# Two more gate units as seven products, the norm weight row from TensorE, u as fp32, cache rows and early loads moved

## The chip, the cores and the metric

The kernel runs on one core of a Trainium2 chip. The metric is the device time of one execution in microseconds (us), as the median of several runs. A core has TensorE (PE in the profile, with its weight loads as PEld), VectorE (DVE), ScalarE (ACT), GpSimd (POOL) and SyncE (SP), which issues most loads; stores are issued by POOL, and data moves over 16 DMA engines.

## The reference

One step of a one-layer streaming encoder over 1,024 prompt frames and 64 sample frames (together T = 1,088 columns), all in fp32:

```
h = rmsnorm(x, g_mix)
cb, cc, ch, q, k, v, ga, gb = split(h @ w_in)   # 3 x 512, 3 x 512, 2 x 1024 columns
u   = cb * causal_conv(cc * ch, state_conv)     # depthwise, width 3
o   = band_attention(q, k, v, rel_bias)         # 8 heads of 64; own 64-frame chunk and 8 before it
mix = sigmoid(ga) * (u @ w_cout) + sigmoid(gb) * (o @ w_ao)
x1  = x + mix @ w_out
y   = rmsnorm(x1 + swiglu(rmsnorm(x1)))         # d_ff = 2816
# further outputs: the new conv state, and the caches of k and v, old rows moved up by 64
```

## The kernel before

**Precision and products.** An fp32 operand is split into a high and a low fp32r half (`split`, L133 to L135: a cast on ACT, then a subtraction on DVE), and a product is three matmuls: high by high, high by low, low by high. Units of 256 columns of w_in are computed in Strassen's way: seven products of half size in place of eight (`STEPS`), each of them 24 matmuls of 272 columns. Class `Unit` loads a unit's raw weights and makes the seven combinations (`prep`), `runner` runs the products, and `results` passes their sums on through copies (`sq`, `sk`, `sg` and so on, L482). The tags A (two places), B and D (one between them, tag BD) are TensorE's PSUM places.

**Stages in order of the program.** (1) The first x tile, the norm weight row `gm_row` and v's weights are loaded; sixteen matmuls on zeros (`wake`, L376) run meanwhile. Each tile of x is squared and summed on ACT (L385), scaled by its norm and by `gm_row` on DVE (L387), turned by TensorE (`xt`, L397), split, and multiplied for v (`pvv`, L430 to L432); q's first unit is begun among these tiles (`q_step`). (2) The list `todo` runs through q0, k0, q1, k1 and cc, ch, cb of both halves, with g0 and g1 (the first four tiles of gate columns, `NG` = 2) among them. `cc_done`, `ch_done` and `cb_done` make the convolution's input `ut`, the convolution (`conv`, whose old contents of `ut` go out as the new conv state) and u, which is written to memory. (3) The other twelve tiles of gate columns (`gates`) are plain products, each four chunks of 24 matmuls (`gate_chunk`, L684 to L686), between the steps of the attention: 8 heads by 9 tiles of queries. One step is the scores `s` (L814, L815), the softmax on DVE (L765) and ACT (L775), for an earlier step the turned weights `t` (L845) and their split `pt`, and for a still earlier one the values `pv` (L871) and their sum (`cb`, `co`, L795 and L796). Scores and turned weights share a PSUM pool of two places. `PER` says how many steps follow a chunk. The last two gate tiles (`BEHIND`) come after the attention and cover the loads of u, o and the row sums r. (4) The merge (`ya` from u, `yb` from o, with the gates), then w_out, the up stage and the down stage, where ACT and DVE work beside long rows of TensorE products.

**What sets the order.** The kernel is written for a scheduler which gives each engine a list of instructions that it works off in order: it takes what is ready by its own estimate, and among that the earlier in the program. Only what is marked so keeps its place in the program (`keep_in_program_order`). An engine that waits at a row holds up all rows behind it on that engine. A buffer of a pool is free when the last reader of its previous contents is done; a load into it is issued only then.

**The rest that the change touches.** The copy of the cache rows (L963) goes from memory to memory on POOL's queue, and the scheduler put its two parts at 8.9 and 42.3 us. u is stored by `cb_done` as two fp32r halves and loaded whole (L926); o and r are loaded in twelve pieces, multiplied (L937) and split. Raw weights share the pool `rpool` with two places.

## Time and profile before

| | |
|---|---|
| median of 3 runs (lowest, highest) | 1539.8 us (1539.04, 1539.97) |
| the profiled execution's own time | 1534.63 us |
| its span, first to last instruction | 1532.8 us |
| mean granted TensorE clock | 0.989 |
| read from and written to memory | 168.86 MB, 89.85 MB |

In a timeline row stand the start, the length, engine, line, operation, output and inputs, the shapes and the number of instructions put together; in brackets is the idle time of that engine ahead of the row and what ended it. A row of a window has, for each engine, its busy time and its number of instructions, then the granted clock, the share of the DMA engines and GB/s. In the chain, a row is a piece of the path that ended last. In a list of groups, behind the bar stand the busy time, the mean of one in ns, and the idle time ahead of them with its cause. The page's second part shows where the program is in time: TensorE is busy in nine tenths or more of nearly every slice but the first.

### The profile page before, as it was taken

How to read it: one execution, taken by the hardware profiler on the slowest of the kernel's cores; microseconds unless marked ns; L12 is line 12 of the kernel's file. 1: busy time of each engine (PE TensorE's matmuls, PEld its weight loads, DVE VectorE, ACT ScalarE, POOL GpSimd, SP SyncE). 2: the span in 40 equal slices, each digit the busy share in tenths (PEclk: the TensorE clock that was granted, in tenths of full speed). 3: DMA queues.
4: the chain of work that ended last, by engine and by line, in shares of the span. 5: the costliest groups of instructions: out<-in, count | busy, mean ns of one | idle time of the engine just before them, and what ended most of it. 6: DMA issues, size and time to landing. Idle time of an engine off the chain costs nothing.

```text
span 1532.8 us, 26063 instructions
## 1 busy us (share of the span) xinstructions
PE 1486.7 (97%) x10002; PEld 1390.1 (91%) x10002; DVE 993.6 (65%) x1893; ACT 686.0 (45%) x1407; POOL 208.3 (14%) x353
## 2 busy tenths in 40 slices
PE   7989998999999999999998999999999999999997
PEld 6789998999999999998888999999999998788886
DVE  6676564555666763666379666666666668857576
ACT  6444432334666663553166444444444445403123
POOL 1234411022222222000200011000010111000000
PEclk9999999999999999999999999999999999999999
DMA  7455522249655627645532344333443438776675
GB/s 251 144 191 188 191 53 87 88 110 302 188 142 158 154 70 259 201 127 161 198 126 74 131 155 154 118 121 124 147 155 141 156 148 309 239 239 225 225 259 199
DMA packets 137868, 257.01 MB, mean 168 GB/s; under 512 B 18432, under 2 KB 76992, under 8 KB 137584
## 3 DMA queue, kind: packets, MB, share of 16 engines
q1 hardware_dynamic: 109264, 167.33, 35.0%
q0 software_dynamic: 27184, 85.40, 15.1%
q10 hardware_dynamic: 1296, 2.62, 0.5%
q8 instruction: 78, 1.28, 0.4%
q14 instruction: 46, 0.38, 0.1%
HBM read 168.86 MB, written 89.85 MB: 169 GB/s over the span
## 4 chain that ended last, share of the span: by engine, by line
PE 84%; DMA 7%; DVE 5%; ACT 3%; issue 1%; SPq 0%; POOL 0%; ACTq 0%; DVEq 0%
PE Aa L261 9%; PE Ab L261 8%; PE A L1480 7%; PE Da L261 4%; PE Db L261 4%; PE D L1480 4%; PE p L686 2%; PE Bb L261 2%; PE Ba L261 2%; PE p L685 2%; PE p L684 2%; PE wo L1045 2%; PE wo L1046 2%; PE wo L1044 2%; PE B L1480 2%; PE Ag L261 2%
## 5 line engine op out<-in xcount | busy, mean ns | idle before, releaser
L1480 PE MATMUL A<-ring,ht 128*128 128x512 f32 x528 | 126.0, 392 | 4.8 <-ACT acc L1490 3.6
L1480 PEld LDWEIGHTS A<-ring,ht 128*128 128x128 f32 x528 | 98.6, 188 | 28.2 <-ACT acc L1490 4.8
L1211 POOL DMA_DIRECT2D h_d<-hq x77 | 41.1, 534 | 412.8 <-DVE hs L135 220.3
L134 ACT CAST ring<-w2r 128x512 fp32r<-128x512 f32 (+1 forms) x78 | 43.6, 589 | 107.4 <-PE A L1480 50.6
L684 PE MATMUL p<-xo,whp 128*128 128x272 f32 x288 | 84.2, 292 | 0.0
L686 PE MATMUL p<-xo,wlp 128*128 128x272 f32 x288 | 83.6, 290 | 0.0
L685 PE MATMUL p<-xo,whp 128*128 128x272 f32 x288 | 83.3, 289 | 0.0
L134 ACT CAST hq<-sa 128x512 fp32r<-128x512 f32 x77 | 47.9, 622 | 75.9 <-DVE sa L1223 57.7
L765 DVE CUSTOM_DVE_ANT_0 p<-s,bias 128x640 f32<-128x640 f32 (+5 forms) x72 | 47.3, 658 | 29.1 <-PE s L815 28.6
L135 DVE TENSOR_TENSOR hq<-sa,hq 128x512 fp32r<-128x512 f32 x77 | 53.0, 689 | 20.0 <-ACT hq L134 19.9
L135 DVE TENSOR_TENSOR wla<-rawa,wha 128x512 fp32r<-128x512 f32 x55 | 37.8, 688 | 41.8 <-ACT wha L134 41.8
L261 PE MATMUL Aa<-mg,wha 128*128 128x272 f32 x352 | 60.3, 293 | 3.9 <-ACT mg L134 3.1
L1480 PE MATMUL D<-ring,ht 128*128 128x512 f32 x264 | 63.9, 394 | 0.0
L1480 PEld LDWEIGHTS D<-ring,ht 128*128 128x128 f32 x264 | 49.5, 188 | 11.9 <-ACT acc L1490 0.4
L261 PE MATMUL Ab<-mg,whb 128*128 128x272 f32 x352 | 58.7, 289 | 0.0
L261 PE MATMUL Ab<-tt,whb 128*128 128x272 f32 x352 | 58.6, 288 | 0.0
L261 PE MATMUL Aa<-tt,wha 128*128 128x272 f32 x352 | 58.6, 288 | 0.0
L134 ACT CAST wha<-rawa 128x512 fp32r<-128x512 f32 x55 | 34.1, 622 | 51.4 <-PE Ab L261 36.8
L135 DVE TENSOR_TENSOR ring<-w2r,ring 128x512 fp32r<-128x512 f32 (+1 forms) x78 | 48.5, 646 | 9.8 <-ACT ring L134 9.6
L261 PEld LDWEIGHTS Aa<-mg,wha 128*128 128x128 f32 x352 | 50.8, 192 | 4.3 <-ACT mg L134 3.4
L684 PEld LDWEIGHTS p<-xo,whp 128*128 128x128 f32 x288 | 54.3, 189 | 0.3
L685 PEld LDWEIGHTS p<-xo,whp 128*128 128x128 f32 x288 | 54.3, 189 | 0.1
(537 smaller groups left out, 4556.5 us busy)
## 6 DMA issues: line engine op xcount, KB each, us to landing
h_d<-hq POOLq DMA_DIRECT2D x77, 512.0 KB, 3.9
ht<-h_d SPq DMA_DIRECT2D x154, 256.0 KB, 3.6
rawa<-in_w_ff SPq DMA_DIRECT2D x11, 1024.0 KB, 5.6
rawb<-in_w_ff SPq DMA_DIRECT2D x11, 1024.0 KB, 4.9
w2r<-in_w_ff SPq DMA_DIRECT2D x11, 1024.0 KB, 4.8
qd<-q_d SPq DMA_DIRECT2D x32, 272.0 KB, 6.2
rawp<-in_w_in SPq DMA_DIRECT2D x6, 1024.0 KB, 8.0
g_d<-gst POOLq DMA_DIRECT2D x24, 256.0 KB, 4.0
```

Of the source, the lines that this page charges most:

```text
L134: act.copy(hi, src)
L135: vec.tensor_tensor(lo, src, hi.bitcast(F32), op=ALU.subtract)
L261: mm(t[:, j, :HN], x[:, k, :], moving(p, l, k, j * HN, HN), start=p in (1, 2, 7) and k == 0 and n == 0, stop=k == 3 and n == 2, skip_group ...
L684: mm(out, a, p, start=g == 0 and k == 0, stop=False)
L685: mm(out, a, q, start=False, stop=False)
L686: mm(out, b, p, start=False, stop=g == last and k == 3)
L765: vec.tensor_tensor_reduce(out=s if len(ps.shape) == 2 else s.rearrange("p (a b) -> p a b", a=2), in0=ps, in1=bias if len(ps.shape) == 2 e ...
L1044: mm(ps, x(k, 0), wh, start=f, stop=False)
L1045: mm(ps, x(k, 0), wl, start=False, stop=False)
L1046: mm(ps, x(k, 1), wh, start=False, stop=e)
L1211: nc.gpsimd.dma_start(h_d[p, c - 1], hq.rearrange("p i l t -> p (i l t)").bitcast(F32))
L1480: mm(t, ht[k][:, j, x], w[:, l], start=p in (1, 2, 7) and k == 0 and n == 0, stop=k == len(ks) - 1 and n == 2, skip_group_check=p in (6, 5 ...
```

## The change

- **Norm weight row.** It is loaded as one row of 4 KB (`gm_one`) instead of 128 copies, multiplied by a column of -0.5 on TensorE (two fp32 matmuls into `gm_ps`, between the wakes) and copied to `gm_row` by ACT. The second x tile is loaded ahead of v's weights.
- **Cache rows.** Their copies are pinned in the up stage.
- **Turned tile 6** gets the PSUM place BD, and q's first two products come one tile later.
- **q1's raw weights** are loaded into a buffer of their own in `cp` (`early`).
- **The convolution** is put into the list of things to be done later, two rounds on for its first half and one for its second.
- **u** is stored and loaded as fp32 and split after the attention. u, o and r are loaded in three chunks of columns for all four row blocks (`chunk`), through two places each; the name `ul` and `ol` share theirs.
- **Gates.** g2 and g3 join `todo` (`NG` = 4). Eight gate tiles stay plain, so `PER` goes from 2.04 to 3.6.

```diff
 C_CB, C_CC, C_CH, C_Q, C_K, C_V, C_GA, C_GB = 0, 512, 1024, 1536, 2048, 2560, 3072, 4096
-PER = 2.04
+PER = 3.6
 WAKE = 16
...
     r_d = dr.tile([NH, T], F32, name="r_d")
-    u_d = dr.tile([4, P, 2, T], F32, name="u_d")
+    u_d = dr.tile([4 * P, T], F32, name="u_d")
     x21_d = dr.tile([P, 2, 4, HT], F32, name="x21_d")
...
     class Unit:
-        def __init__(self, src, nm):
+        def __init__(self, src, nm, place=None):
             self.nm = nm
             self.pool = ws
-            self.raw = rpool.tile([P, KD, 2 * P], F32, tag="raw", name=f"raw{nm}")
+            self.raw = (place or rpool).tile(
+                [P, KD, 2 * P], F32, tag="raw", name=f"raw{nm}", bufs=1 if place else 2
+            )
             nc.sync.dma_start(self.raw, src.rearrange("(k p) n -> p k n", p=P))
...
-    def unit_in(n):
+    def unit_in(n, place=None):
         nm, at, _ = todo[n]
-        return Unit(w_in[:, at : at + 256], nm)
+        return Unit(w_in[:, at : at + 256], nm, place)
...
+        gm_one = ph.tile([P, D], F32, tag="x", name="gm_one", bufs=3)[:1]
         load_x(HORDER[0])
-        gm_row = ph.tile([P, D], F32, name="gm_row", bufs=1)
         gm = ins["g_mix"][0]
-        nc.scalar.dma_start(gm_row, bass.AP(tensor=gm.tensor, offset=gm.offset, ap=[[0, P], [1, D]]))
-        pool_e.tensor_scalar(gm_row, gm_row, -0.5, None, op0=ALU.mult)
+        nc.scalar.dma_start(gm_one, bass.AP(tensor=gm.tensor, offset=gm.offset, ap=[[D, 1], [1, D]]))
+        load_x(HORDER[1])
         wv_raw = []
...
             wv_raw.append(raw)
-            load_x(HORDER[half + 1])
+        load_x(HORDER[2])
         wv = []
...
         wake = psS.tile([P, 512], F32, tag="mm", name="wake")
+        minus_half = ph.tile([P, 2, 4, P], F32, tag="kept", name="minus_half", bufs=4)[:1, 0, 0]
+        vec.memset(minus_half, -0.5)
+        gm_ps = bank2("A", "gm_ps")
         for i in range(WAKE):
+            if i == 4:
+                for j in range(2):
+                    mm(gm_ps[:, j], minus_half, gm_one[:, j * 512 : (j + 1) * 512], start=True, stop=True)
             mm(wake, zero[:, :P], zero, start=True, stop=True)
+        gm_row = ph.tile([P, D], F32, name="gm_row", bufs=1)
...
-        def norm(i):
+        def norm(i, also=None):
...
             act.activation(junk[:n], xt[:n], AF.Square, accum_out=ssq[:n])
+            if also:
+                also()
             r = norm_factor(ph, ssq[:n], n, f"m{i}")
...
             xg = xts.pop(i)
-            pt = bank2("A", f"xt_{i}").rearrange("p a (b t) -> p a b t", t=P)
+            pt = bank2("BD" if i == 6 else "A", f"xt_{i}").rearrange("p a (b t) -> p a b t", t=P)
             for hf in range(2):
...
-        norm(HORDER[0])
+        norm(HORDER[0], lambda: act.copy(gm_row, gm_ps.rearrange("p a b -> p (a b)")))
         norm(HORDER[1])
...
                 q_step = runner(unit, todo[0][2])
-            if n in (5, 6):
-                q_step.products(n - 5)
+            if n in (6, 7):
+                q_step.products(n - 6)
...
         return snap.rearrange("p j n -> p (j n)")
-
-    def staged(nm):
-        return sp.tile([P, 2, HT], F32R, tag="st", name=nm)
...
             if ended[r] == 2:
-                conv(r)
+                late.append([2 - r, lambda: conv(r)])
...
                 vec.tensor_tensor(x[:, a : a + n], x[:, a : a + n], cvo[r][:, col(t) : col(t) + n], op=ALU.mult)
-            st = staged(f"su{c2}_{r}{h}")
-            split(st[:, 0], st[:, 1], x)
+            i = 2 * c2 + r
             for a, t, n in places(h):
-                nc.gpsimd.dma_start(u_d[2 * c2 + r, :, :, t : t + n], st[:, :, a : a + n].bitcast(F32))
+                nc.gpsimd.dma_start(u_d[i * P : (i + 1) * P, t : t + n], x[:, a : a + n])
...
             todo.append((f"{nm}{c2}", base + 256 * c2, (c2, n)))
-    NG = 2
+    NG = 4
+    for m in range(2, NG):
+        todo.append((f"g{m}", C_GA + 256 * m, gate_out(2 * m)))
...
     cvp = k_step = None
+    early = {2: unit_in(2, cp)}
     for n, (nm, at, done) in enumerate(todo):
...
         if n + 1 < len(todo):
-            nxt_unit = unit_in(n + 1)
+            nxt_unit = early.pop(n + 1, None) or unit_in(n + 1)
         for si in range(len(STEPS)):
...
     ob = Acts([uo.tile([P, 2, 4, T], F32R, name="ob")])
-    for i in range(4):
-        nc.sync.dma_start(u.t[0][:, :, i, :].bitcast(F32), u_d[i])
-    with tc.tile_pool(name="ol", bufs=3, reuse_waits="tile") as olp:
-        for i in range(4):
-            for c, (o, n) in enumerate(CH):
-                t = olp.tile([P, 384], F32, tag="ol", name=f"ol{i}_{c}")
-                nc.sync.dma_start(t[:, :n], o_d[i * P : (i + 1) * P, o : o + n])
-                rb = olp.tile([P, 384], F32, tag="rb", name=f"rb{i}_{c}")
-                for j in range(2):
-                    nc.sync.dma_start(
-                        rb[j * HD : (j + 1) * HD, :n], r_d[2 * i + j : 2 * i + j + 1, o : o + n].to_broadcast([HD, n])
-                    )
-                vec.tensor_tensor(t[:, :n], t[:, :n], rb[:, :n], op=ALU.mult)
-                split(ob.at(0, i, o, n), ob.at(1, i, o, n), t[:, :n])
+    with tc.tile_pool(name="ol", bufs=2, reuse_waits="tile") as olp:
+
+        def chunk(src, o, n, nm):
+            t = olp.tile([P, 4, 384], F32, tag="ol", name=f"{nm}_{o}")[:, :, :n]
+            nc.sync.dma_start(t, src[:, o : o + n].rearrange("(i p) t -> p i t", p=P))
+            return t
+
+        for c, (o, n) in enumerate(CH):
+            t = chunk(u_d, o, n, "ul")
+            split(u.four(0, 0, o, n), u.four(0, 1, o, n), t)
+            t = chunk(o_d, o, n, "ol")
+            rb = olp.tile([P, 4, 384], F32, tag="rb", name=f"rb_{o}")[:, :, :n]
+            for j in range(2):
+                nc.sync.dma_start(
+                    rb[j * HD : (j + 1) * HD],
+                    bass.AP(
+                        tensor=r_d.tensor, offset=r_d.offset + j * T + o, ap=[[0, HD], [2 * T, 4], [1, n]]
+                    ),
+                )
+            vec.tensor_tensor(t, t, rb, op=ALU.mult)
+            split(ob.four(0, 0, o, n), ob.four(0, 1, o, n), t)
         for n in range(len(gates) - BEHIND, len(gates)):
...
     wo_raw = []
-    for nm in ("k", "v"):
-        src = ins[f"cache_{nm}"].rearrange("t h d -> t (h d)")
-        nc.gpsimd.dma_start(outs[f"cache_{nm}_sample"][: CACHE - TS], src[TS:])
...
     unit = ub
+    for nm in ("k", "v"):
+        src = ins[f"cache_{nm}"].rearrange("t h d -> t (h d)")
+        tc.keep_in_program_order(nc.gpsimd.dma_start(outs[f"cache_{nm}_sample"][: CACHE - TS], src[TS:]))
     for n in range(1, len(names)):
...
```

ACT's order at the start, rows 4 to 13, before and after; `junk` is the Square of an x tile, `wvh` the high half of v's weights, `kept` and `xo` come from a turned x tile:

```order
4 L385 ACTIVATE junk,ssq_142<-x_109 128x1024
5 L148 ACTIVATE normm_144<-normm_144 128x1
6 L134 CAST wvh_176<-wv_114 128x512
7 L134 CAST wvh_180<-wv_114 128x512
8 L134 CAST wvh_184<-wv_114 128x512
9 L134 CAST wvh_188<-wv_114 128x512
10 L385 ACTIVATE junk,ssq_151<-x_116 128x1024
11 L148 ACTIVATE normm_153<-normm_153 128x1
12 L134 CAST wvh_192<-wv_118 128x512
13 L134 CAST wvh_196<-wv_118 128x512
```

```order
4 L394 ACTIVATE junk,ssq_147<-x_110 128x1024
5 L148 ACTIVATE normm_150<-normm_150 128x1
6 L394 ACTIVATE junk,ssq_157<-x_113 128x1024
7 L456 COPY gm_row<-gm_ps 128x1024
8 L148 ACTIVATE normm_159<-normm_159 128x1
9 L134 CAST wvh_182<-wv_115 128x512
10 L134 CAST wvh_186<-wv_115 128x512
11 L134 CAST wvh_190<-wv_115 128x512
12 L162 COPY kept_175<-xt_166 128x512
13 L134 CAST xo_99<-xt_166 128x4x128
```

The two Squares and the copy of the row now stand ahead of all casts of v's weights, and the first turned tile's copy and cast ahead of the second half of these weights (wv_117).

SP's queue around the load of q1's raw weights, before (rawq_1042) and after (rawq_813); `bt` and `ct` are the bias and cache rows that are loaded behind the last x tile:

```order
13 L354 DMA x_525<-in_x_prompt 128x1024
14 L594 DMA bt<-in_bias_ext 8x768
15 L582 DMA ct_1357<-in_cache_k 128x512
16 L582 DMA ct_1467<-in_cache_k 128x512
17 L595 DMA bias_e<-bt 8x768
18 L194 DMA rawq_1042<-in_w_in 128x8x256
```

```order
13 L356 DMA x_531<-in_x_prompt 128x1024
14 L601 DMA bt<-in_bias_ext 8x768
15 L196 DMA rawq_813<-in_w_in 128x8x256
16 L602 DMA bias_e<-bt 8x768
17 L589 DMA ct_1363<-in_cache_k 128x512
18 L589 DMA ct_1473<-in_cache_k 128x512
```

The load moved ahead of the cache rows and has no earlier reader to wait for.

TensorE in the third head's attention, from the scores of tile 6 to those of tile 7, before and after; `p` are the gates' plain products:

```order
1419 L814 MATMUL s_6_4817<-kd_4309,qd_0_4312 128x320
1420 L815 MATMUL s_6_4817<-kd_4309,qd_1_4315 128x320
1421 L814 MATMUL s_6_4817<-kd_4309,qd_0_4312 128x320
1422 L815 MATMUL s_6_4817<-kd_4309,qd_1_4315 128x320
1423 L845 MATMUL t_4_4826<-ident,p_4_4748 128x128 x5
1424 L871 MATMUL pv_3_4835<-pt_1_4757,vd_4325 128x512 x3
1425 L871 MATMUL pv_3_4835<-pt_1_4757,vd_4325 128x2x128
1426 L684 MATMUL p_0_4873<-xo_99,whp_00_4532 128x272
1427 L814 MATMUL s_7_4847<-kd_4309,qd_0_4312 128x320
```

```order
1425 L696 MATMUL p_3_5193<-x_4100,wlp_00_4313 128x272
1426 L694 MATMUL p_3_5193<-x_4100,whp_00_4312 128x272
1427 L695 MATMUL p_3_5193<-x_4100,whp_00_4312 128x272
1428 L696 MATMUL p_3_5193<-x_4100,wlp_00_4313 128x272
1429 L694 MATMUL p_3_5193<-xo_101,whp_01_4316 128x272
1430 L695 MATMUL p_3_5193<-xo_101,whp_01_4316 128x272
1431 L855 MATMUL t_4_5081<-ident,p_4_5031 128x128 x5
1432 L881 MATMUL pv_3_5090<-pt_1_5040,vd_4664 128x512 x3
1433 L881 MATMUL pv_3_5090<-pt_1_5040,vd_4664 128x2x128
1434 L696 MATMUL p_3_5193<-xo_101,wlp_01_4317 128x272
1435 L694 MATMUL p_3_5193<-xo_101,whp_01_4316 128x272
1436 L824 MATMUL s_7_5129<-kd_4648,qd_0_4651 128x320
```

Before, such a step has one plain matmul in it here, and others (the next of this head) have some twenty; after, each has about eight. Over the whole attention, from the first scores to the last row sum, there are some 885 of them before and 574 after.

## The prediction

> **What bounds the kernel now.** I read the page's busy shares and its chain first, then the rows of TensorE's timeline, looking for places where an idle time stands in brackets behind a row, and last the windows over single stages.
>
> ```profile
> PE 1486.7 (97%) x10002; PEld 1390.1 (91%) x10002; DVE 993.6 (65%) x1893; ACT 686.0 (45%) x1407; POOL 208.3 (14%) x353
> ...
> PE 84%; DMA 7%; DVE 5%; ACT 3%; issue 1%; SPq 0%; POOL 0%; ACTq 0%; DVEq 0%
> ```
>
> TensorE is busy for 1486.7 of 1532.8 us, and 84% of the chain is its own work. So time can go in three ways: fewer TensorE instructions, closing the 46 us in which it stands idle, and raising the clock behind idle places. The profiled run took 1534.63 us, 1.8 more than its span and 5.2 less than the median, 1539.8. I sum differences against the profiled run and take them off the median, since nothing says that the change moves the distance between the two.
>
> **The start** (norm row, order of the loads, cache rows). TensorE's timeline, then other engines' rows of the same time:
>
> ```profile
> 1.48 6.26 PE L376 MATMUL wake<-zero 128*128 128x512 f32 x16 [1.48 <-DVE zero L373]
> 13.12 1.97 PE L397 MATMUL xt<-ident,x 128*128 128x128 f32 x8 [5.38 <-DVE x L387]
> 17.62 0.50 PE L430 MATMUL pvv<-wvh,xo 128*128 128x512 f32 x1 [0.38 <-ACT xo L134]
> 26.10 1.06 PE L397 MATMUL xt<-ident,x 128*128 128x128 f32 x8 [0.75 <-DVE normm L149]
> ```
>
> ```profile
> 5.88 1.06 ACT L385 ACTIVATE junk<-x 128x1024 bf16<-128x1024 f32 x1 [3.22 <-DMA x<-in_x_prompt]
> 6.14 2.78 POOL L360 TENSOR_SCALAR gm_row<-gm_row 128x1024 f32<-128x1024 f32 x1 [3.73 <-DMA gm_row<-in_g_mix]
> 9.97 1.90 DVE L135 TENSOR_TENSOR wvl<-wv,wvh 128x512 fp32r<-128x512 f32 x3 [1.87 <-ACT wvh L134]
> 11.41 1.05 ACT L385 ACTIVATE junk<-x 128x1024 bf16<-128x1024 f32 x1
> 11.79 1.28 DVE L387 SCALAR_TENSOR_TENSOR x<-x,normm,gm_row 128x1024 f32<-128x1024 f32 x1
> 15.33 1.14 ACT L134 CAST wvh<-wv 128x512 fp32r<-128x512 f32 x2 [1.97 <-DMA wv<-in_w_in]
> 16.50 0.59 ACT L162 COPY kept<-xt 128x512 f32<-128x512 f32 x1
> ```
>
> Before, the row is ready at 6.14 + 2.78 = 8.92, the scaling stands on DVE behind three wvl subtractions (to 11.8), and the cast that frees the first v matmul stands on ACT behind two casts that wait for wv's second half (15.33). After, the ACT order is Square of x0, Square of x1, the copy that makes the row, then three casts of wv. Square of x0 ends at about 7 with its accumulator read; Square of x1, whose load is now second, adds 1.05 to 1.4, and the copy of 1024 columns, which the trace does not show, at least 0.59 (half its columns, row at 16.50) and at most 2 x 0.59 = 1.2; I take 1.1, as the Square of 1024 columns takes. The row is there at 9.6 to 9.7. DVE then scales x0 at once (1.28): x0's turn starts at about 11.0 instead of 13.12. Two casts or copies of 0.59 behind its first half put the first v matmul at 13 instead of 17.62. The two fp32 matmuls that make the row are not in the trace: at least the 0.39 of a wake matmul (6.26 / 16), and, if fp32 costs four times that, 1.6 each, 3.2 together. They lie among the sixteen wakes, which have nothing to do before 11.0, and so cost nothing; they even shorten the idle time ahead of the first turn. To these 4.6 us comes the wait of 0.75 at 26.10 for the next tile's norm, whose inputs are earlier too. The term: **-5.4**. Its ends: -2, when wv's second half still lands at 15.3 and the second group of casts waits for it, and -7.5. The queue now carries 1 MB less of other work in those microseconds (the row's 512 KB broadcast, and a cache copy of 896 KB, below), so I take the nearer end to the latter.
>
> **q's two units** (PSUM place of the turned tile, products one tile later, q1's raw weights early). Rows of TensorE's timeline; of the chain; and windows whose next to last figures are granted clock and DMA share:
>
> ```profile
> 63.92 1.38 PE L397 MATMUL xt<-ident,x 128*128 128x128 f32 x8 [3.18 <-DVE x L387]
> 91.09 0.77 PE L261 MATMUL Aq<-xo,whq 128*128 128x272 f32 x4 [1.85 <-ACT whq L134]
> 107.92 0.77 PE L261 MATMUL Aq<-xo,whq 128*128 128x272 f32 x4 [2.65 <-DVE sq L482]
> ```
>
> ```profile
> 71.21 3.00 PE Bq L261 x24
> 77.70 0.87 PE xt L397 x8
> 96.59 9.86 DMA rawq<-in_w_in
> 107.15 0.73 DVE sq L482
> ```
>
> ```profile
> 91.10:95.10 4.00, 3.91 (x17) 3.54 (x18) 4.00 (x7) 2.02 (x4) 2.09 (x4) 0.59 0.81 296
> 107.90:112.60 4.70, 4.68 (x25) 4.68 (x26) 4.37 (x7) 1.85 (x4) 1.46 (x2) 0.64 0.63 207
> 1299.00:1304.00 5.00, 3.26 (x13) 2.17 (x12) 4.71 (x8) 4.71 (x10) 0.00 (x0) 1.00 1.04 408
> ```
>
> Between the last two turned tiles (63.92 and 77.70) the old order has a product of 24 matmuls and 35 of v, some 11 us; the new one has 6 of v and a product, 4.4 us. So the work that ACT and DVE do on the last tile starts some 6 us earlier, more than the 1.85 us that TensorE waited at 91.09, and what is late next is DVE's own queue. The second wait hangs on a load: q1's raw weights were issued only at 96.59, when q0's buffer came free, and landed 9.86 later; DVE stood at the subtraction that reads them, with the one behind it (107.15) that frees TensorE's PSUM. With a buffer of its own the load is the 15th row of SP's queue instead of the 18th and waits for nothing of q0; its 9.86 us then lie beside the last tiles of v, far ahead of 107. I take both waits away, 1.85 + 2.65 = 4.5, and the low clock behind each, 4.0 x 0.41 = 1.6 and 4.7 x 0.36 = 1.7: **-7.8**. Ends: -3, if DVE's queue is late in both places, and -8.5. The wait of 3.18 at 63.92 is for the last x load, which the change leaves where it was: 0.
>
> The row at 1299 has waits of the same size, and its clock stays 1.00; so whether a wait of some 2 us lowers the clock is not fixed by its length. The Trainium skill ("TensorE: Matmul & The Clock Gate", Part 1: The HAM clock gate) puts the halving behind at least one idle window of some 3.4 us that runs freely. By that rule neither wait here should have lowered the clock, and the 3.3 us of the two stretches would stay, for a sum 3.3 higher; the two windows at 0.59 and 0.64 speak against it, the one at 1299 for it.
>
> **The convolution's wait** (it is issued two steps later at most).
>
> ```profile
> 237.78 0.06 DVE L527 MEMSET ut<- 128x2 f32 x1 [8.48 <-DMA out_state_conv_sample<-ut]
> 241.90 1.19 PE L261 MATMUL Ag<-xo,whg 128*128 128x272 f32 x4 [4.08 <-DVE sg L482]
> 241.90:246.50 4.60, 4.60 (x24) 4.60 (x25) 1.78 (x3) 0.00 (x0) 2.18 (x4) 0.63 0.56 178
> out_state_conv_prompt<-ut POOLq DMA_DIRECT2D x4, 1.0 KB, 12.2
> ```
>
> DVE stands 8.48 us at a memset, until a store of the old contents has landed, and TensorE waits 4.08 behind it, with 4.6 x 0.37 = 1.7 of low clock. In the order after, the memset has moved by one row and the stores by as little. A store of 1 KB takes 12.2 us by the median, and nothing shortens it. I take **-0.5**; the ends are 0 and -5.8.
>
> **Gates and attention.** Two more units of 256 columns as seven products: 14 products of 24 matmuls more, 14 x 3.00 = 42.0 us. In return 16 plain chunks of 24 matmuls go.
>
> ```profile
> 364.80:584.40 219.60, 216.99 (x1579) 202.45 (x1578) 150.24 (x376) 149.05 (x353) 49.32 (x91) 1.00 0.54 151
> 584.40:606.30 21.90, 21.90 (x177) 21.87 (x176) 4.11 (x9) 5.28 (x14) 4.85 (x9) 1.00 1.00 356
> L765 DVE CUSTOM_DVE_ANT_0 p<-s,bias 128x640 f32<-128x640 f32 (+5 forms) x72 | 47.3, 658 | 29.1 <-PE s L815 28.6
> L135 DVE TENSOR_TENSOR pt<-t,pt 128x640 fp32r<-128x640 f32 (+2 forms) x64 | 41.8, 652 | 10.1 <-ACT pt L134 9.6
> DVE p L765 <- PE s L815: 28.6, 31, 2.2
> ACT pt L134 <- PE t L845: 17.3, 32, 1.3
> ```
>
> In the second window TensorE does nothing but plain chunks: 21.90 / 177 = 0.124 us a matmul. So 16 x 24 x 0.124 = 47.5 go, 42.0 come: **-5.5**. That is TensorE alone. The plain chunks are also what it does while ACT and DVE turn scores into weights. Of the first window's matmuls some 885 are such filler; after, by the order, 574. The attention's own work is 219.6 - 885 x 0.124 = 109.9 us, 1.5 for each of 72 steps; with 574 x 0.124 = 71.2 of filler the window would be 181 us, 2.5 a step instead of 3.05. DVE's 150.2 and ACT's 149.1 in the window shrink only by the share of the gates (a third of some 11 and 24 us), to 146 and 141: from 68% to 81% and 78% of the window. Both stay below full, and DVE's waits for scores (28.6 us) say that it is TensorE that is late today. But each step is a ring: turn the weights (five transposes), ACT casts, DVE subtracts (0.652), and only then is the PSUM place free for the next but one. I add **+3** for places where this ring is late, between 0 and +10. After the last step 98 filler matmuls (12 us) are left instead of 176 (21.9).
>
> **u and the merge.** u's high and low halves were loaded as written; now u is loaded once, as fp32, and split.
>
> ```profile
> u<-u_d SPq DMA_DIRECT2D x4, 1088.0 KB, 9.4
> 609.58 4.17 DMA rb<-r_d
> 613.88 0.57 DVE ol L937
> L684 PE MATMUL yb<-ob,whm 128*128 128x384 f32 (+1 forms) x96 | 32.2, 337 | 3.4 <-ACT ob L134 3.4
> 615.00:619.00 4.00, 3.96 (x13) 3.97 (x14) 2.49 (x6) 0.97 (x2) 0.00 (x0) 0.50 0.57 150
> ```
>
> Today the merge waits 3.4 us for o and loses 4.0 x 0.50 = 2.0 by the clock behind it. After, half of u's 4.4 MB is not loaded, and 40 DMAs become 12; but the work on a chunk of four rows (1536 columns, so about 4 x 0.57 = 2.3 us on DVE for the product and as much for each subtraction, less what starting each costs) runs through two buffers that u and o share. The loads of the second and third chunk wait for the first's, and only 12 us of filler cover them. I take **0**, with -5 and +5 as ends: the old waits end, and others of that size come. The eight casts and subtractions that split u before go from engines that are not the bound.
>
> The cache rows move into the up stage:
>
> ```profile
> out_cache_k_sample<-in_cache_k POOLq DMA_DIRECT2D x1, 896.0 KB, 7.0
> ```
>
> Two copies of 7 us each beside a stage of hundreds of microseconds, ahead of POOL's first stores there: 0, and at worst one store late by their issue, +1.
>
> **The sum:** -5.4 - 7.8 - 0.5 - 5.5 + 3 + 0 = -16.2, which gives 1518.4 for a run like the profiled one and **1523.6** for the median.
>
> **The rivals.**
>
> The pace of attention (the other side). If a step takes what it takes today, 3.05 us, because the ring of ACT, DVE and two PSUM places sets it and the filler only fills, the window stays at 219.6 instead of 184: +35.6, so 1559.2. The point from which the change loses is 184 + 16.2 = 200 us, 2.78 us a step. Against it speak 216.99 busy of 219.60 on TensorE and DVE's 28.6 us of waiting for scores; for it, the 81% of DVE in a ring with two places. In full I give it 0.08. In part (2.65 to 2.75 a step) it gives 7 to 14 us more, 1531 to 1537: 0.16.
>
> The convolution's wait closes too, if the stores land as early as DVE's 8.48 us would let them, and the start takes its far end: -5.3 - 2, so 1516.3. The two-step delay and a queue that is less full speak for it, the 12.2 us of a store against it: 0.18.
>
> The edit at the start does not do what it says, because wv's load and not the row set the first tiles: the ACT row that waits for wv at 15.33 is for it. The start then gives -2, and the time is 1527. Likewise DVE late at q1 (-3 in place of -7.8) gives 1528. Together 0.14.
>
> The low clock at both q waits stays, as the rule on the clock would have it: 1526.9. 0.04.
>
> **How the numbers follow.** The forecast has 0.40. All cases between 1518 and 1529, the forecast, the start, q and the clock, hold 0.58, and the far side around 1516 0.18. The range of 1512 to 1537 leaves out the full pace rival and a little at each end. A measurement of this kernel tells some 0.2% (3.1 us) from no change: faster by more holds everything but the pace rival and the upper end of its partial form, 0.86; same 0.06; slower 0.08.
>
> **What would show it.** Right: the first v matmul near 13 us; no wait over 1 us ahead of the two Aq rows, and clock 1.00 behind them; 14 more products of 3.00; the window from the first score to the last row sum near 184 us, with TensorE busy in nearly all of it; wait and low clock at g's fifth product still there. Wrong: an attention window over 190 us, with idle time of TensorE ended by ACT's pt or DVE's p; a first wait in the merge above 6 us; an x scaling that stands behind wv's subtractions as before.

## The result, and the profile after

| | before | after |
|---|---|---|
| median (lowest to highest, runs) | 1539.88 us (1539.04 to 1541.82, 4) | 1523.84 us (1519.76 to 1526.03, 4) |
| the profiled execution's own time, span | 1534.63, 1532.8 | 1526.03, 1524.3 |

The ratio is 0.9897, with a 95% interval of 0.9881 to 0.9912: 16.0 us less, where 16.2 were forecast. The spans of the two traces differ by only 8.5 us. Both kernels were therefore profiled a second time (E1 and E2, below); there the spans are 1538.5 and 1524.4, 14.1 apart. The first profile of before was a fast draw. The sum came out right, but not all of its terms, so that it came out within 0.2 us is luck.

Busy shares and chain of the page after:

```profile
PE 1486.5 (98%) x9958; PEld 1386.0 (91%) x9958; DVE 999.7 (66%) x1891; ACT 683.4 (45%) x1392; POOL 201.6 (13%) x352
...
PE 89%; DVE 4%; DMA 4%; ACT 2%; issue 1%; POOL 0%; ACTq 0%; DVEq 0%; SPq 0%; POOLq 0%
```

TensorE is as busy as before (1486.5 against 1486.7): what fell is its idle time. Its share of the chain rose from 84% to 89%, and DMA's fell from 7% to 4%.

TensorE's timeline after: the start, the last x tile, q0's third and last products (the places of the waits of 1.85 and 2.65 before), g's fifth product, and the merge's two waits for o:

```profile
4.35 3.78 PE L383 MATMUL gm_ps<-gm_one,minus_half 1*128 1x512 f32 x4
8.06 4.63 PE L384 MATMUL wake<-zero 128*128 128x512 f32 x10
12.49 2.60 PE L408 MATMUL xt<-ident,x 128*128 128x128 f32 x16
15.38 0.50 PE L441 MATMUL pvv<-wvh,xo 128*128 128x512 f32 x1 [0.29 <-ACT xo L134]
...
60.38 1.09 PE L408 MATMUL xt<-ident,x 128*128 128x128 f32 x8 [2.39 <-DVE x L398]
...
85.68 0.77 PE L263 MATMUL Aq<-xo,whq 128*128 128x272 f32 x4 [0.24 <-ACT whq L134]
...
98.38 0.66 PE L263 MATMUL Aq<-xo,whq 128*128 128x272 f32 x4
...
231.46 1.28 PE L263 MATMUL Ag<-xo,whg 128*128 128x272 f32 x4 [4.66 <-DVE sg L493]
...
600.28 0.44 PE L694 MATMUL yb<-ob,whm 128*128 128x384 f32 x1 [4.21 <-ACT ob L134]
...
612.45 0.63 PE L694 MATMUL yb<-ob,whm 128*128 128x320 f32 x1 [3.98 <-ACT ob L134]
```

Windows after: first scores to last row sum, the plain products behind it, the merge, the time around q0's last products, and the time behind g's wait:

```profile
396.20:577.20 181.00, 180.21 (x1274) 164.88 (x1273) 140.45 (x367) 135.90 (x330) 41.20 (x77) 1.00 0.61 166
577.20:589.40 12.20, 12.20 (x100) 12.20 (x99) 5.12 (x5) 5.03 (x9) 3.75 (x7) 1.00 0.63 180
589.40:699.90 110.50, 101.59 (x578) 99.65 (x577) 64.77 (x124) 50.87 (x110) 1.07 (x2) 0.94 0.49 143
86.00:104.00 18.00, 17.81 (x141) 17.55 (x140) 16.47 (x27) 10.08 (x18) 8.51 (x14) 1.00 0.86 268
231.50:236.00 4.50, 4.50 (x21) 4.50 (x21) 1.74 (x3) 0.00 (x0) 2.17 (x4) 0.52 0.55 175
```

The attention's window is 38.6 us shorter, with TensorE busy in 180.21 of 181.00. The merge took 110.5 us, where the page before has 102.9 between the rows that bound it:

```profile
352.73 0.29 PE L684 MATMUL p<-xo,whp 128*128 128x272 f32 x1
...
606.41 0.34 PE L684 MATMUL ya<-u,whm 128*128 128x384 f32 x1
...
709.28 0.63 PE L1044 MATMUL wo<-wo_hi,mg 128*128 128x512 f32 x2
```

These three rows (first plain product, first ya, first wo) exist in every trace, so they cut the program into four stages. Each entry is a length in us; 42.1 for the 14 further products of after, which stand in its first stage, is moved to the second.

| stage | before | before again (E1) | after | after again (E2) | first pair | second pair | forecast |
|---|---|---|---|---|---|---|---|
| start to first plain product | 352.7 | 359.2 | 342.0 | 343.8 | -10.7 | -15.4 | -13.7 |
| to first ya: gates, attention | 253.7 | 253.4 | 247.4 | 247.1 | -6.3 | -6.3 | -2.5 |
| to first wo: merge | 102.9 | 103.1 | 110.6 | 109.7 | +7.7 | +6.6 | 0 |
| to the end | 823.5 | 822.7 | 824.4 | 823.9 | +0.9 | +1.2 | 0 |
| span | 1532.8 | 1538.5 | 1524.3 | 1524.4 | -8.5 | -14.1 | -16.2 |

Two terms were off and partly cancelled: attention gained more than was forecast, and the merge lost what was forecast as nothing. Together these two stages are no faster than before (6.3 gained, 7.7 and 6.6 lost): the whole gain lies ahead of the first plain product.

### The profile page after: what moved, and what is told of

It is laid out like the page before. It is cut to its first block, busy times and chain, and to the rows that moved or that the text cites. A ratio compares the mean times of both kernels' runs of the same rounds, so it can differ in the third digit from the quotient of the medians.

```text
span 1524.3 us, 25952 instructions
## 1 busy us (share of the span) xinstructions
PE 1486.5 (98%) x9958; PEld 1386.0 (91%) x9958; DVE 999.7 (66%) x1891; ACT 683.4 (45%) x1392; POOL 201.6 (13%) x352
## 4 chain that ended last, share of the span: by engine, by line
PE 89%; DVE 4%; DMA 4%; ACT 2%; issue 1%; POOL 0%; ACTq 0%; DVEq 0%; SPq 0%; POOLq 0%
PE Aa L263 9%; PE Ab L263 8%; PE A L1497 7%; PE Da L263 4%; PE Db L263 4%; PE D L1497 4%; PE Ag L263 3%; PE Bb L263 2%; PE Ba L263 2%; PE t L855 2%; PE p L696 2%; PE wo L1059 2%; PE p L695 2%; PE p L694 2%; PE wo L1060 2%; PE wo L1058 2%
## 5 line engine op out<-in xcount | busy, mean ns | idle before, releaser
L696 PE MATMUL p<-xo,wlp 128*128 128x272 f32 x192 | 56.8, 296 | 0.0
L695 PE MATMUL p<-xo,whp 128*128 128x272 f32 x192 | 56.6, 295 | 0.0
L694 PE MATMUL p<-xo,whp 128*128 128x272 f32 x192 | 56.6, 295 | 0.0
L785 ACT ACTIVATE p<-p,mx 128x640 f32<-128x640 f32 (+5 forms) x72 | 50.8, 706 | 7.1 <-DVE mx L775 6.6
L1509 DVE TENSOR_TENSOR acc<-A,acc 128x512 f32<-128x512 f32 x52 | 35.7, 687 | 25.6 <-PE A L1497 25.4
```

The source lines that it names most:

```text
L694: mm(out, a, p, start=g == 0 and k == 0, stop=False)
L695: mm(out, a, q, start=False, stop=False)
L696: mm(out, b, p, start=False, stop=g == last and k == 3)
L785: act.activation(s, s, AF.Exp, bias=mx, scale=-1.0, accum_out=sm)
L1509: vec.tensor_tensor(o, t, o, op=ALU.add)
```

## The experiments

All but E1 are timed; ratios are to the kernel before, and "changed" is the changed kernel (1523.8, again 1526.1). The kernel before, timed beside them on other occasions, had medians of 1540.8 to 1542.2, where the table has 1539.9. So medians of two experiments that differ by some 2 us are not told apart.

**E1 and E2: both kernels once more.**

> The kernel before, unchanged, profiled once more. The two traces on record differ by 8.5 us of span (9.5 up to the last computation), the medians by 16.0, and the profiled run of before (1534.63) lies 4.4 under the lowest unprofiled one. Theory A: that run was a low draw of a quantity that varies from run to run. Then this profile's own time lies between 1536 and 1542, and its timeline shows in one or two places 3 to 7 us that the first trace does not have. Rival B: profiled runs of this kernel are 5 us shorter for a reason of their own. Then it comes out within 1533 to 1536 again, with the same timeline to 0.5 us at the wait at g's fifth product and at the merge.

> The changed kernel, unchanged, profiled once more, with times. Theory A (draws): its runs spread by 4 to 6 us as before (1519.8 to 1526.0), and the places where this trace and the first one part are low clock or waits of TensorE that come and go. Rival B: the profile lies within 1 us of the first (1526.0) and the spread is in the unprofiled runs alone.

E1 took 1540.25 us, and E2 1526.13 (1523.62 to 1526.23; 0.9896, 0.9875 to 0.9917). In E1 TensorE's row at g's fifth product has the wait 6.52 where the first trace had 4.08, and the wait for the last x tile is 4.54 instead of 3.18; with the clock behind them (0.50 each time, 0.63 in the first trace) that is most of the 6.5 us by which its first stage is longer. Theory A holds for before. E2's profile is within 0.2 us of the first, as rival B had it, though places moved in it (5.89 at g, 1.22 at the last x tile, a new wait of 2.43 that ends at 319.6 us).

**E3: eleven matmuls on zeros.**

```diff
-WAKE = 16
+WAKE = 11
```

> Eleven matmuls on zeros instead of sixteen. In the trace of the changed kernel the first turned tile starts when the last of them ends (12.69 us), though its scaled x is there at 10.49. Theory: they bound the start now; with five fewer (5 x 0.46 = 2.3 us) the first turned tile starts at 10.5 and the first v matmul at 13.2 instead of 15.4, 2.2 us less in all, if the clock stays up. Rival 1: the clock is then low through the first tiles, as it was before the change, which costs 1.5 to 2 us: no gain. Rival 2: v's weights are late instead (their second half lands after 14): the first v matmul comes earlier, and the third turned tile at 25.9 all the same.

1526.25 us (0.9901, 0.9881 to 0.9921): no gain. TensorE's start in E3, and the window over its first turned tiles:

```profile
4.35 2.02 PE L383 MATMUL gm_ps<-gm_one,minus_half 1*128 1x512 f32 x4
6.29 1.44 PE L384 MATMUL wake<-zero 128*128 128x512 f32 x5
9.54 1.94 PE L408 MATMUL xt<-ident,x 128*128 128x128 f32 x8 [1.80 <-DVE normm L149]
...
13.52 0.77 PE L441 MATMUL pvv<-wvh,xo 128*128 128x512 f32 x1
```

```profile
9.50:13.50 4.00, 3.51 (x16) 3.17 (x17) 3.73 (x7) 3.39 (x7) 0.00 (x0) 0.50 0.91 319
```

The first turn starts 2.95 us earlier than in the changed kernel (9.54, 12.49), with no wake ahead of it, and the first v matmul 1.86. But the clock is 0.50 there: eight turns took 1.94, where sixteen took 2.60. At cc's first product 1.5 us of gain are left (161.29; E2: 162.82), and they were gone behind g's wait, which ended at 230.55 (E2: 229.98). So the low clock (rival 1) explains the smaller part and the wait at g the larger. The two fp32 matmuls and the wakes behind them also ran faster here than in the changed kernel; E11 has the same eleven wakes without that.

**E4: a third buffer for the pieces of u and o.**

```diff
-            t = olp.tile([P, 4, 384], F32, tag="ol", name=f"{nm}_{o}")[:, :, :n]
+            t = olp.tile([P, 4, 384], F32, tag="ol", name=f"{nm}_{o}", bufs=3)[:, :, :n]
```

> Three buffers instead of two for the pieces of u and o in the merge. In the trace of the changed kernel the load of o's second piece is issued at 591.78, when the subtraction on o's first ends, lands 5.06 later, and TensorE waits 4.21 for it and 3.97 for the third piece, with low clock behind. Theory: the two shared buffers cause both waits; with a third the second piece is loaded some 7 us earlier and its wait goes (4.2, and 1 to 2 of low clock); the third piece's wait shrinks by 1 to 4: 6 to 9 us less in the span from the first ya to the first wo matmul (110.5). Rival: the chain of work on a piece (product 1.76, cast 1.47, subtraction 1.76 on two engines) is what is late, and the waits stay within 1 us.

1519.87 us (0.9867, 0.9835 to 0.9898). The load of o's second piece in the chain of the changed kernel, then the two waits in E4:

```profile
591.78 5.06 DMA ol<-o_d
```

```profile
596.19 0.44 PE L694 MATMUL yb<-ob,whm 128*128 128x384 f32 x1 [1.52 <-ACT ob L134]
606.21 0.41 PE L694 MATMUL yb<-ob,whm 128*128 128x320 f32 x1 [1.79 <-ACT ob L134]
```

In E4 this load is issued at 582.72, 9 us earlier. The waits shrink from 4.21 and 3.98 to 1.52 and 1.79, and the merge from 110.5 (109.7 in E2) to 105.0: 5.5 or 4.6 us, less than the 6 to 9 expected. The buffers cause the larger part of the two waits; what is left of them still ends with the cast of ob, as in the rival.

**E5: the new conv state stored from copies.** DVE copies the two columns to a small tile `keep`, and the store reads that tile.

```diff
+                keep = cvp.tile([P, 2], F32, tag=f"ks{r}{nm}", name=f"ks{c2}{r}{nm}")
+                vec.tensor_copy(keep, u[:, a : a + 2])
-                    outs[nm][:, i * P : (i + 1) * P].rearrange("j p -> p j"), u[:, a : a + 2]
+                    outs[nm][:, i * P : (i + 1) * P].rearrange("j p -> p j"), keep
```

> The changed kernel, but the two columns that go out as the new conv state are first copied by DVE to small tiles of their own (eight copies of two columns, some 0.06 us each), so that the memset of the next ut waits for no store. In four traces these stores land 8.6 to 18.9 us after their issue, and TensorE waits 4.07, 6.53 (before) and 4.66, 5.89 us (after) at g's fifth product, with 4.5 us of low clock behind. Theory: this landing sets the place, before and after alike, and is the largest part of what varies from run to run: the wait goes (4.7 to 6.9 us, and some 2 us of clock), the median is 6 to 9 us under the changed kernel's, and the runs spread by less than 3 us. Rival: DVE is late there anyhow, with the raw weights of the next unit (cc) or the loads of the old conv state: the wait shrinks to 2 to 4 us and the time by under 3.

1520.97 us (0.9870, 0.9847 to 0.9893), 3 to 5 under changed. The memset waits no more, and yet TensorE waits 4.74 us. The chain of E5, then DVE's row:

```profile
204.18 21.59 DMA rawcc<-in_w_in
```

```profile
225.86 0.69 DVE L216 TENSOR_TENSOR sf_in<-rawcc 128x512 f32<-128x512 f32 x1 [6.86 <-DMA rawcc<-in_w_in]
```

DVE now stands at the raw weights of cc, whose load was issued at 204.18, beside four stores and two loads of the conv state, and took 21.6 us. A second wait had hidden behind the first. That is the rival's cause, though the wait is longer than its 2 to 4 us.

**E6: q1's raw weights late.** `early = {}` in place of `early = {2: unit_in(2, cp)}`.

> The changed kernel with q1's raw weights in the shared pool again, loaded when q0's place is free. Theory: the wait at q1's second product comes back, 2 to 3 us with some 1.7 of low clock, 4 to 5 us up to the first product of cc. Since the wait at g's fifth product ends by stores and not by TensorE, a part of it is swallowed there: 1 to 4 us in the end. Rival: the wait was cured by DVE's earlier work on the last tile, and the load is in time anyhow: under 0.5 us at q1.

1532.02 us (0.9939, 0.9915 to 0.9963): 6 to 8 slower than changed. The wait is ahead of q0's last product (the expectation calls it q1's second); it ends when DVE gets past q1's raw weights. DVE's row, TensorE's row and the window behind it:

```profile
98.52 0.69 DVE L216 TENSOR_TENSOR sf_in<-rawq 128x512 f32<-128x512 f32 x1 [6.39 <-DMA rawq<-in_w_in]
```

```profile
99.90 1.27 PE L263 MATMUL Aq<-xo,whq 128*128 128x272 f32 x4 [4.00 <-DVE sq L493]
```

```profile
99.90:104.50 4.60, 4.60 (x25) 4.60 (x26) 4.34 (x7) 1.90 (x4) 1.46 (x2) 0.66 0.63 201
```

The wait is back, 4.00 with 4.6 x 0.34 = 1.6 of clock. Nothing was swallowed at g: the wait there was 7.19, longer than E2's.

**E7: turned tile 6 in place A, q's products a tile earlier.** `bank2("A", ...)` for every tile, and `if n in (5, 6): q_step.products(n - 5)`.

> The changed kernel with turned tile 6 in PSUM place A again and q's first two products one tile earlier. Theory: the last tile's chain starts some 6 us later against TensorE, the wait ahead of q0's third product (1.85 before) comes back with low clock behind it: 3 to 4 us up to cc's first product, and 0 to 4 in the end. Rival: only the earlier load of q1's weights mattered, and no wait over 0.5 us appears there.

1527.10 us (0.9901, 0.9876 to 0.9927). The place of the wait of 1.85 before, in E7:

```profile
82.57 0.77 PE L263 MATMUL Aq<-xo,whq 128*128 128x272 f32 x4 [0.24 <-ACT whq L134]
```

No wait: the rival. E6, which keeps the new place, has no wait over 0.2 there either. So either edit alone removes that wait, and beside the earlier load the place is worth nothing that can be told.

**E8: two gate units, as before.** `NG = 2`, `PER = 2.04`.

> The changed kernel with two gate units as seven products, twelve plain tiles and the old number of steps for a chunk (2.04). Theory: 42.1 us of products go and 16 x 24 plain matmuls come, 6.3 us more from the first plain product to the first of ya (253.5 instead of 205 + 42.1), as in the traces; the window from the first scores to the last row sum is again 219 to 220. In the end 4 to 7 us slower than the changed kernel. Rival: attention with less filler has a loss that the traces hide elsewhere, for instance in the merge: then the merge is 3 us or more faster than the 109.7 to 110.5 us of the changed kernel, since more filler (22 us instead of 12) covers its loads, and the end differs by less than 3.

1523.46 us (0.9887, 0.9862 to 0.9911): as fast as changed. From the first plain product to the first ya (339.33 to 594.77) it takes 255.4, 8.1 more than 247.3; the merge (594.77 to 697.05) takes 102.3, 8 less than 110.5. Of the merge's two waits for o only one of this size is left:

```profile
608.63 0.63 PE L694 MATMUL yb<-ob,whm 128*128 128x320 f32 x1 [3.61 <-ACT ob L134]
```

The rival was right: what two more units gain in attention, the merge gives back for want of cover.

**E9: the old path of u, with q1 late** (both do not fit in memory otherwise): two stored halves, the old twelve pieces; to be read against E6.

> u stored as two halves again and u, o and r loaded in the old pieces, and, since its memory is then short, q1's raw weights loaded late too; all else as changed. To be compared with the run that has q1's weights late alone (1532.0, merge from first ya to first wo matmul 109.7). Theory: the merge's loss comes from the cover, 12 us of plain products after the last step in place of 22, so the old pieces lose as much or more: merge 109 to 116, time within 3 of 1532 or above it. Rival: it comes from the new loop itself (long pieces, two shared buffers): merge 102 to 104, and the time 5 to 7 us under 1532.

1542.51 us (0.9997, 0.9982 to 1.0012), 10.5 more than E6. The merge is as long as E6's (110.8 against 111.4), as the theory had it, though by other waits: 3.77 us for a row of the gates (`ga`) and three of 0.8 to 1.3 for o. The 10.5 us were lost elsewhere, which neither said. ACT's and TensorE's rows in E9, at the end of cb's second unit and the start of g2:

```profile
361.05 0.64 ACT L134 CAST su<-cb 128x544 fp32r<-128x544 f32 x1 [5.11 <-DMA u_d<-su]
361.60 0.61 ACT L134 CAST whg<-rawg 128x512 fp32r<-128x512 f32 x1
362.12 0.60 ACT L249 COPY sg<-Ag 128x544 f32<-128x544 f32 x1
```

```profile
328.08 1.27 PE L263 MATMUL Ag<-xo,whg 128*128 128x272 f32 x4 [3.89 <-DVE sg L493]
362.77 0.77 PE L263 MATMUL Ag<-xo,whg 128*128 128x272 f32 x4 [2.12 <-ACT sg L249]
```

The cast of u's last block waits for a store of an earlier one, and the copy that frees TensorE's place stands behind it: 2.12 us, which no other run has. The wait of 3.89 is at the fifth product of g's second unit, where DVE stands at the next raw weights; E2, E6 and E7 have 2.43, 0.84 and 2.90 there, so it is not the old path's alone. With low clock behind both (0.50 and 0.63 over 4.6 us) the first plain product is 9.4 us later than in E6. So u as fp32 saves at least the stall of 2.12 when two more units follow cb, and its memory is what q1's early load lives in; how much of the rest is its doing stays open.

**E10: the conv state stored as rows.** The columns are kept in one tile, turned once, and stored in the merge as 2 x 8 rows of 512 bytes.

```diff
+                vec.tensor_copy(keep[:, m, :, i], u[:, a : a + 2])
...
+    nc.tensor.transpose(tk[:16, :P], keep.rearrange("p m j i -> p (m j i)"), ident)
+    act.copy(rows, tk[:16, :P])
+        nc.gpsimd.dma_start(outs[nm].rearrange("j (i p) -> (j i) p", p=P), rows[8 * m : 8 * m + 8])
```

> The changed kernel, but the columns of the new conv state are kept in a small tile, turned once by TensorE in the merge and stored as two sets of eight rows of 512 bytes, in place of sixteen stores... in all eight pairs of 4-byte columns. In the run with copies (stores from tiles of their own) the wait at g's fifth product stayed at 4.74 us, since the raw weights of cc then took 21.6 us to land (8 and less elsewhere) beside these stores. Theory: the stores of 4-byte elements themselves hold up the loads that run beside them; without them cc's weights land in under 12 us, the wait at g's fifth product is under 1 us, and so is the one near 316 us; the median is 8 to 11 us under the changed kernel's 1525, and the runs spread by less. Rival: the loads of the old conv state, also 4-byte elements, which stay, or the order of the queue are the cause: rawcc takes 18 us or more again and the wait stays over 3 us.

1517.52 us (0.9838, 0.9821 to 0.9855), 6 to 9 under changed. The landings of the raw weights of cc, in a view by tile, of E2 and of E10:

```profile
DMA to landing us min/median/max: 8.2/14.3/20.5
```

```profile
DMA to landing us min/median/max: 5.4/7.2/9.0
```

Both waits, at g and near 316, are gone; no row in this stretch waits over 1.01. TensorE's row at g's fifth product in E10:

```profile
225.10 0.66 PE L264 MATMUL Ag<-xo,whg 128*128 128x272 f32 x4
```

The loads of the old state, 4-byte elements too, are still there. So it is the stores. Whether it is their small elements is argued, not shown: E10 changes their form and moves them to the merge at once. The expected smaller spread did not come: 1515.17 to 1520.90.

**E11: E10, E4 and E3 together.**

> The changed kernel with the turned conv state, three buffers for u and o in the merge, and eleven matmuls on zeros. Theory: the gains add, since no late store now fixes the end of the first stages: 8 to 11 from the stores, 5 from the merge, 1 to 2 from the start, so 1508 to 1512. Rival: what the start gains is lost at the next wait (the last x tile, at 58 us): 1511 to 1514.

1516.09 us (1512.04 to 1517.59; 0.9818, 0.9801 to 0.9834), the fastest, but only 1.4 under E10, less than either expected. In the profiled runs its merge is 103.4 against 109.4, so E4's gain is there. It was lost again at the start, whose stage is 2.7 us longer, and behind the merge, 3.6 us longer. TensorE's start in E11:

```profile
8.05 2.50 PE L385 MATMUL wake<-zero 128*128 128x512 f32 x5
10.64 1.94 PE L409 MATMUL xt<-ident,x 128*128 128x128 f32 x8
```

With five wakes fewer and the rest as slow as in the changed kernel, the first turn starts 1.85 us earlier and right behind the last wake: the wakes bound the start. But eight turns take 1.94 again, and the wait at the last x tile is 2.46 (E10: 1.21). In the down stage the same wait had another clock behind it. TensorE's row and window in E10, then in E11, and a longer window of each:

```profile
1294.63 1.66 PE L1502 MATMUL A<-ring,ht 128*128 128x512 f32 x6 [1.81 <-ACT acc L1512]
1294.60:1299.20 4.60, 4.57 (x20) 3.80 (x21) 0.80 (x3) 1.29 (x3) 0.00 (x0) 1.00 0.89 307
1280.00:1300.00 20.00, 16.11 (x67) 12.10 (x68) 16.07 (x28) 10.92 (x22) 0.00 (x0) 1.00 0.79 281
```

```profile
1293.39 2.54 PE L1502 MATMUL A<-ring,ht 128*128 128x512 f32 x6 [1.81 <-ACT acc L1512]
1293.40:1298.00 4.60, 4.60 (x13) 3.65 (x14) 0.00 (x0) 1.30 (x3) 0.00 (x0) 0.63 0.82 309
1280.00:1300.00 20.00, 18.05 (x65) 13.75 (x64) 14.49 (x25) 9.89 (x20) 0.00 (x0) 0.83 0.68 246
```

Over the 20 us, E11 loses 20 x 0.17 = 3.4 by the clock, which is most of the 3.6.

**E12: two gate units with three buffers.**

> Two gate units as seven products with the old number of steps for a chunk, and three buffers for u and o in the merge; to be compared with the run that has four units and three buffers (1519.9, merge 105.0) and with the two that have two buffers (four units 1523.8 to 1526.1, merge 109.7 to 110.5; two units 1523.5, merge 102.2). Theory: with two units the merge had little to gain (at most the wait of 3.6 and its clock, 1 to 5 us), so this is within 98 to 102 us in the merge, and 8 us longer from the first plain product to the first ya, once the 42.1 us are taken off: 1520 to 1524, that is 1 to 4 us slower than four units with three buffers; the two more units are worth what the merge does not take. Rival: also here the two come out equal within 1 us, and the units are worth nothing in any form.

1522.87 us (0.9863, 0.9849 to 0.9878): by the medians 3.0 over E4's 1519.87, by the ratios (0.9867 for E4) none. The merge took 103.6, not the 98 to 102 expected, so with two units the third buffer gains nothing there. From the first plain product to the first ya it is 7.1 us longer than E4, in the merge 1.4 shorter. So the two stages speak for the two more units once there are three buffers, but the times do not tell it from the rival.

## Why the prediction was right in sum, point by point

- **Start, -5.4: mis-sized.** The step that failed is that the two fp32 matmuls "lie among the sixteen wakes ... and so cost nothing". With 0.39 for a wake and 3.2 for the two, all of it ends at 10.9, just ahead of the 11.0 for x. They took 3.78 us, and a wake took 0.46 to 0.49: the last ended at 12.69, though the x for the first turn was there at 10.49. The first v matmul came at 15.38, not 13: 2.2 instead of 4.6, and with the 0.75 at 26.10 about -3.0. E11 shows that the wakes bound it. The wait for the last x tile, put at 0, fell by 0.8 in the first pair and by 3.3 in the second, which no term of the forecast had.
- **q's units, -7.8: right in size, half wrong in cause.** Both waits and the low clock are gone. From the first product of k0 to the first of cc it is 90.5 us before and 83.1 after: -7.4 (second pair: -7.7). The step on the turned tile failed as a reason: E7 keeps its old place, has no wait and takes the same 83.1. E6, without the early load, takes 88.7: the early load carries 5.6, and the rest goes with either edit.
- **Convolution, -0.5: right in that it stays.** The wait at g was 4.08 and 6.52 before, 4.66 and 5.89 after. That "nothing shortens it" held for the change; E10 removes it.
- **Gates, -5.5, and the ring of attention, +3: the second was wrong.** The stage gained 6.3 in both pairs, and the window is 181.0, the 181 worked out without stalls. DVE's 140.45 in it is 78%, where 81% was expected, and its ring was not late. The pace rival had no part in it.
- **The merge, 0: wrong by 6.6 to 7.7**, beyond the end of +5 that was given. The step that failed is "the old waits end, and others of that size come": the waits for o were 4.21 and 3.98 where there had been one of 3.39. Their cause was named there (the loads wait for the two shared buffers, and 12 us of filler cover them) and then taken as even. E4 and E8 show both halves: a third buffer gives 4.6 to 5.5 us back, and nearly twice the cover gives 8.
- **Cache rows, 0: right.** Behind the merge the stages differ by 0.9 to 1.2, of which no more than 0.2 lies ahead of the down stage.
- **Low clock behind the waits of q:** gone with the waits, so the rival from the Trainium skill ("TensorE: Matmul & The Clock Gate", Part 1: The HAM clock gate) did not come true here. But its free-running window would fit what E10 and E11 show: one and the same wait of 1.81 us is followed by full clock in one run and by 0.63 in the other. No run here shows a window. That waits far under 3.4 us lower the clock at all (1.85 to 0.59 before, 1.81 to 0.63 in E11) is not what its rule says.

The cancelling errors were +2.4 (start) and about +7 (merge) against some 4 (attention) and, in the second pair, 3.3 at the last x tile. That such errors cancel to 0.2 is luck. One premise failed as well: the prediction took the distance between the profiled run and the median as fixed, but that run lay 5.2 under the median before and 2.2 over it after. Had the median fallen by the first pair's 8.5, the forecast of 1523.6 would have been 7.7 too low.

**Open:** what makes the runs of one kernel differ by up to 8 us (E9), and E3's four by only 1. The stores of the conv state are not most of it (E10's spread). The clock behind short waits can be (3.4 us in the 20 us of E11), but no count over many runs was made.

## What to carry to other kernels

Filler for one stage is cover for the next: before taking work out of a stage, look at which loads it hides behind it, and price those loads with their buffers. Take a wait that ends by DMA apart twice, since a second transfer may stand behind the first with the same end. And a trace is one draw: profile the kernel before twice before a sum is made to a few us.

## What the runs showed of the hardware

The stores of the new conv state hold up the loads beside them. In the twelve traces that have them, four stores of 1 KB in 4-byte elements, with two loads of that kind, stand beside the load of 1 MB of cc's second unit, and it lands 17.7 to 22.6 us after its issue; in E10 and E11, without the stores, after 9.0 and 8.6. The Trainium skill ("DMA: Bandwidth & Descriptors", Specifications) asks for 512 bytes for a transfer at line rate, and says (Issuing engines are not separate DMA queues) that transfers of all engines interleave on the same 16. The landings agree with the first: 8.6 to 18.9 us for the 1 KB in 4-byte elements, 3.5 to 4.9 us for E10's rows of 512 bytes. That such rows would delay no load was not tried, since E10 moved them to the merge.

The two matmuls of one fp32 row by 512 columns appear as four instructions; they took 0.95 us each in the changed kernel (3.78 / 4) and 0.51 in E3 (2.02 / 4), and the wakes behind them 0.46 and 0.29 each. E11, with as many wakes as E3, has the slow figures, so it is not their number. The granted clock does not tell the two apart: in the windows it is 1.00 over the first 12.5 us of the changed kernel. It is 1.00 also from 9.50 to 13.50 in E11, where eight turns take the 1.94 us that they take at 0.50 in E3. So in the first microseconds the lengths of the rows are the better sign, and why they differ was not tried.
